# The first q group of the last layer is rounded behind the first splits of the folded projection, and the attention weights lie head by head

## The chip, the cores and the metric

The kernel runs on one core of a Trainium2 chip. The metric is the device time of one execution in microseconds; the time before is the median of three runs.

## What is computed

A two-layer encoder over 272 positions (256 tokens and 16 meta tokens) of width 2048, in float32. Per layer:

```python
h = rmsnorm(x)
q, k, v, f, ga, gf = split(h @ w_in)
q, k = rope_2d(rmsnorm(q)), rope_2d(rmsnorm(k))     # 8 heads of 128, 2 key/value heads
a = attention(q, k, v) @ w_attn_br                  # bidirectional, 4 q heads share one k and v
s = real(fft2(f groups)) @ w_four                   # per group of 128 channels
x = x + (sigmoid(ga) * a + sigmoid(gf) * s) @ w_out
x = x + w_down(silu(dwconv3(rmsnorm(x) @ w_up_gate)) * (rmsnorm(x) @ w_up_val))
```

## The kernel before

**Products in two parts.** A float32 operand is used as a rounded high part and a low part, the difference. A weight chunk of 128 x 1024 (512 KB) is loaded by SyncE into one of four `raw` buffers (L264), ScalarE casts it to the high part `wh` (L306), VectorE subtracts to get the low part `wl` (L308), and TensorE multiplies high by high, high by low and low by high (L377 to L379). `wh` and `wl` have three buffers each. `next_split` and `advance` keep the splits two chunks ahead of the matmuls.

**Work between the matmuls.** Whatever isn't a weight product (norms, rotation, attention) is written as generators that are pushed on a list, `shadow`. After every second product of a group, `step` wakes at most one generator whose count is up; `yield n` sets that count, so a larger n puts the rest of a generator later among the matmuls. A scheduler may then move instructions on an engine; inside `tc.manual_schedule(...)` the engines named keep the written order.

**The last layer's q groups.** `group((l, "q", i), ...)` makes the projection of q group i (two heads). `head_evac` (L927) takes it out of PSUM: the squares on ScalarE (L935, tile `qps`) and the scaled values on VectorE (L936, tile `qp`). `swap` (L946) copies the halves of each head to `qs` by four DMAs. `q_stage` (L1037) takes the sums of squares (the copy L1047 to `sqm` and the transposes L943) and then calls `rope` (L952): two products with sine and cosine (L953, L954), their sum (L955), the rounding to the high part on ScalarE (L956), one `yield`, and the low part on VectorE (L958).

**The folded projection.** Behind q group 1 of the last layer stands `folded_f` (L832), under `manual_schedule` for VectorE and ScalarE. It runs over 16 chunks of a folded weight (`raw<-fw`). For chunk k it first issues the high and low splits of the chunk ahead, then the matmuls of chunk k: for each of four groups g and two halves, high part (L869) and low part (L873), and for the first group two small matmuls besides (L872). The four groups take eight PSUM banks; the third and fourth use the banks of the q groups, the fourth those of q group 1, and its chunk 0 is done within chunk 1 (the list `kg`). Every third chunk up to k = 11 VectorE also makes the folded activations for later chunks (`fold_sum`, `fold_low`). Chunks 0 and 1 are split during the last two chunks of q group 1, chunk 2 at k = 0, chunk 3 at k = 1.

**Attention.** `attention(kv, rq)` handles four heads of one key/value head. Its scores are exponentiated (L1103), normalised (`pn`, L1111 and L1112), transposed on TensorE (L1120) and written, rounded, to `PH` (L1133) and the low part to `PL` (L1134); the third key block holds the meta tokens' remainder, with its low part in rows 32 to 47 (L1136). A head's weights are three key blocks of 272 positions in `PH` and two in `PL`. `values(h)` multiplies them by v: for each of two blocks L1141 (`PH`), L1142 (`PL`) and L1143 (`PH` with the low part of v), and then L1144. In the last layer a head's values are done one round later than the next head's first weights are written. Which earlier write a matmul waits for is found by the framework from the ranges of the tile that the two touch.

## Time and profile before

| | us |
|---|---|
| three runs, median (lowest to highest) | 2510.45 (2509.78 to 2512.84) |
| the profiled execution | 2510.57 |
| its span, first to last instruction | 2508.5 |
| TensorE matmul busy | 2496.9 |
| VectorE busy | 1987.7 |
| ScalarE busy | 1341.0 |
| GpSimd busy | 205.4 |

The span is what the trace covers; the profiled execution's own time is 2.07 us longer. Busy times of different engines overlap. A row of the timeline gives start and duration in microseconds from the start of the span, the engine (PE is TensorE, DVE VectorE, ACT ScalarE, POOL GpSimd, SP SyncE), the source line, the operation, and output and inputs by the program's names; brackets hold the idle time of the engine before it and what ended it. A row of the waits gives the waiting engine and line, what it waited for, and the total, the number of times and the longest. The folded projection runs from 1364.2 to 1399.05 us of the span, and the last layer's attention ends at about 1530.

### The profile page before, as it was taken

What the parts mean: (1) busy time and instruction counts of PE and PEld (TensorE: products, weight loads), DVE (VectorE), ACT (ScalarE), POOL (GpSimd) and SP (SyncE); (2) the same over time, 40 slices, a digit from 0 to 9 for tenths busy, and PEclk for the clock granted to TensorE, in tenths of its full rate; (3) what the DMA queues carried; (4) which work ended last, traced back from release to release, by engine and by line L of the source; (5) the groups of instructions that cost most, each with busy time, mean ns of one, the idle gap of its engine ahead of it and who ended that gap; (6) DMA issues with size and microseconds to landing.
All of it is one profiled execution on the core that took longest, in us unless ns stands there. A gap on an engine that the chain in (4) does not pass through costs nothing.

```text
span 2508.5 us, 47931 instructions
## 1 busy us (share of the span) xinstructions
PE 2496.9 (100%) x18848; PEld 2416.3 (96%) x18848; DVE 1987.7 (79%) x3155; ACT 1341.0 (53%) x1913; POOL 205.4 (8%) x394
## 2 busy tenths in 40 slices
PE   9999999999999999999999999999999999999999
PEld 8999999999999999999999999999988899999887
DVE  7687866778878667888778887666888787898898
ACT  5455434554444334444445555444676665666665
POOL 0000000012212222222200000000000000000000
PEclk9999999999999999999999999999999999999999
DMA  7544557879999999999975647888878887788897
GB/s 249 165 152 164 190 192 245 265 260 377 393 335 383 404 385 377 384 391 389 391 276 197 200 152 236 268 260 273 245 266 294 295 292 237 262 284 291 278 302 272
DMA packets 194803, 706.85 MB, mean 282 GB/s; under 512 B 22145, under 2 KB 27393, under 8 KB 194321
## 3 DMA queue, kind: packets, MB, share of 16 engines
q1 hardware_dynamic: 146768, 517.09, 58.9%
q0 software_dynamic: 46368, 184.57, 21.3%
q8 instruction: 147, 2.41, 0.4%
q10 hardware_dynamic: 1440, 2.13, 0.2%
q14 instruction: 80, 0.65, 0.1%
HBM read 623.32 MB, written 111.15 MB: 293 GB/s over the span
## 4 chain that ended last, share of the span: by engine, by line
PE 98%; DVE 1%; DMA 1%; issue 0%; POOL 0%; ACT 0%; ACTq 0%; DVEq 0%; POOLq 0%
PE ps_p L1455 14%; PE ps_ug L379 7%; PE ps_ug L377 7%; PE ps_ug L378 7%; PE ps_d L379 3%; PE ps_uv L379 3%; PE ps_uv L377 3%; PE ps_uv L378 3%; PE ps_d L377 3%; PE ps_d L378 3%; PE ps_ga L377 2%; PE ps_o L379 2%; PE ps_o L377 2%; PE ps_ga L378 2%; PE ps_ga L379 2%; PE ps_gf L377 2%
## 5 line engine op out<-in xcount | busy, mean ns | idle before, releaser
L306 ACT CAST wh<-raw 128x1024 fp32r<-128x1024 f32 (+1 forms) x961 | 998.3, 1044 | 891.9 <-PE ps_ug L378 194.4
L308 DVE TENSOR_TENSOR wl<-raw,wh 128x1024 fp32r<-128x1024 f32 (+1 forms) x961 | 1158.9, 1217 | 392.3 <-ACT wh L306 382.0
L377 PE MATMUL ps_ug<-xHL,wh 128*128 128x272 f32 (+1 forms) x1408 | 400.4, 285 | 0.0
L379 PE MATMUL ps_ug<-xHL,wl 128*128 128x272 f32 (+1 forms) x1408 | 398.7, 284 | 0.0
L378 PE MATMUL ps_ug<-xHL,wh 128*128 128x272 f32 (+1 forms) x1408 | 398.5, 283 | 0.0
L377 PEld LDWEIGHTS ps_ug<-xHL,wh 128*128 128x128 f32 x1408 | 264.9, 188 | 3.2
L378 PEld LDWEIGHTS ps_ug<-xHL,wh 128*128 128x128 f32 x1408 | 264.5, 188 | 3.2
L379 PEld LDWEIGHTS ps_ug<-xHL,wl 128*128 128x128 f32 x1408 | 264.3, 188 | 1.1 <-DVE wl L308 0.4
L1455 PE MATMUL ps_p<-wh,opnd 128*128 128x512 f32 x816 | 222.1, 392 | 0.0
L379 PE MATMUL ps_uv<-xHL,wl 128*128 128x272 f32 x704 | 201.9, 287 | 0.0
L379 PE MATMUL ps_d<-gHL,wl 128*128 128x272 f32 x704 | 201.7, 287 | 0.0
L377 PE MATMUL ps_uv<-xHL,wh 128*128 128x272 f32 x704 | 201.3, 286 | 0.0
L377 PE MATMUL ps_d<-gHL,wh 128*128 128x272 f32 x704 | 201.1, 286 | 0.0
L378 PE MATMUL ps_uv<-xHL,wh 128*128 128x272 f32 x704 | 200.6, 285 | 0.0
L378 PE MATMUL ps_d<-gHL,wh 128*128 128x272 f32 x704 | 200.6, 285 | 0.0
L1455 PEld LDWEIGHTS ps_p<-wh,opnd 128*128 128x128 f32 x816 | 148.3, 188 | 28.7 <-ACT wh L306 0.2
L377 PE MATMUL ps_ga<-xHL,wh 128*128 128x272 f32 (+1 forms) x512 | 147.8, 289 | 0.0
L540 DVE TENSOR_TENSOR wi<-wi,wi 128x512 f32<-128x512 f32 x224 | 147.0, 685 | 0.0
L377 PE MATMUL ps_gf<-xHL,wh 128*128 128x272 f32 (+1 forms) x512 | 146.7, 287 | 0.0
L379 PE MATMUL ps_o<-mH,wl 128*128 128x272 f32 (+1 forms) x512 | 145.8, 285 | 0.0
L377 PE MATMUL ps_o<-mH,wh 128*128 128x272 f32 (+1 forms) x512 | 145.5, 284 | 0.0
L378 PE MATMUL ps_ga<-xHL,wh 128*128 128x272 f32 (+1 forms) x512 | 145.4, 284 | 0.0
(379 smaller groups left out, 5952.9 us busy)
## 6 DMA issues: line engine op xcount, KB each, us to landing
raw<-in_w_up SPq DMA_DIRECT2D x288, 512.0 KB, 6.5
raw<-in_w_in SPq DMA_DIRECT2D x191, 512.0 KB, 3.8
raw<-in_w_down SPq DMA_DIRECT2D x88, 512.0 KB, 7.0
wi<-in_w_dn POOLq DMA_DIRECT2D x80, 512.0 KB, 9.4
ft<-wi POOLq DMA_DIRECT2D x80, 512.0 KB, 7.7
raw<-ft SPq DMA_DIRECT2D x80, 512.0 KB, 4.7
raw<-in_w_out SPq DMA_DIRECT2D x64, 512.0 KB, 4.3
raw<-fv SPq DMA_DIRECT2D x64, 512.0 KB, 4.8
```

The costliest lines, as they stand in the source:

```text
L306: nc.scalar.copy(h[:, a:b], r[:, a:b])
L308: nc.vector.tensor_tensor(lo[:, a:b], r[:, a:b], h[:, a:b].bitcast(F32), op=ALU.subtract)
L377: nc.tensor.matmul(o, h[:, c, sl], a, start=kt == 0, stop=False)
L378: nc.tensor.matmul(o, h[:, c, sl], b, start=False, stop=False)
L379: nc.tensor.matmul(o, lo[:, c, sl], a, start=False, stop=kt == nk - 1)
L540: tt = lambda *v, **kw: tc.keep_in_program_order(nc.vector.tensor_tensor(*v, **kw))
L1455: nc.tensor.matmul(ps[h], x, w[:, 512 * h:512 * h + 512], start=fresh and (s_, q) in BEGIN and first, stop=(s_, q) in END and end, skip_gr ...
```

## The change

Two edits.

The first concerns q group 0 of the last layer alone. `rope` is cut in two: `turn` is the part up to the sum, and `q_stage` calls only `turn` for that group, after `yield 10` in place of `yield 6`, and leaves the tiles in `hold["q0"]`. The rounding and the low part are issued in `folded_f` at k = 0, behind the splits of the chunk ahead. All other groups call `rope` as before, which now calls `turn`.

The second changes the order of the dimensions of `PH` and `PL` in both layers: (block, head, position) becomes (head, block, position). Shapes, sizes and the instructions are the same.

```diff
                     if k < KT - 1:
                         for j in ahead:
                             split_w(j, 0, CW, "l")
+                    if k == 0:
+                        hp, H, L = hold.pop("q0")
+                        nc.scalar.copy(H, hp)
+                        nc.vector.tensor_tensor(L, hp, H.bitcast(F32), op=ALU.subtract)
                     if k == 13:
                         nc.scalar.activation(warm, mhalf[:, 0:1], AF.Exp)
...
-            def rope(hp, qs, H, L):
+            def turn(hp, qs):
                 tc.keep_in_program_order(nc.vector.tensor_tensor(qs, qs, bc2(sin), op=ALU.mult))
                 tc.keep_in_program_order(nc.vector.tensor_tensor(hp, hp, bc2(cos), op=ALU.mult))
                 nc.vector.tensor_tensor(hp, hp, qs, op=ALU.add)
+
+            def rope(hp, qs, H, L):
+                turn(hp, qs)
                 nc.scalar.copy(H, hp)
                 yield 1
                 nc.vector.tensor_tensor(L, hp, H.bitcast(F32), op=ALU.subtract)
...
-                yield 6 - j
-                yield from rope(qp, qs, qH[kv][:, sl, :], qL[kv][:, sl, :])
+                if last and i == 0:
+                    yield 10
+                    turn(qp, qs)
+                    hold["q0"] = qp, qH[kv][:, sl, :], qL[kv][:, sl, :]
+                else:
+                    yield 6 - j
+                    yield from rope(qp, qs, qH[kv][:, sl, :], qL[kv][:, sl, :])
...
-                PH = PHf.rearrange("p (b h t) -> p b h t", b=3, h=4)
-                PL = PLf[:, :2 * 4 * T].rearrange("p (b h t) -> p b h t", b=2, h=4)
+                PH = PHf.rearrange("p (h b t) -> p b h t", b=3, h=4)
+                PL = PLf[:, :2 * 4 * T].rearrange("p (h b t) -> p b h t", b=2, h=4)
```

How the written order falls out on the engines. The rows give line, operation, output and inputs, and the size of the output; the lines of the changed kernel are its own, up to 13 higher.

VectorE at the seam of q group 1 and the folded projection. `wl_16824` is the low part of chunk 0, `wl_16859` that of chunk 1, `wl_16901` of chunk 2 and `wl_16921` of chunk 3; L953 to L958 rotate and round q group 0 (`q_16735` is its low part), and L936 takes q group 1 out of PSUM. Before:

```order
L308 TENSOR_TENSOR wl_16824<-raw_16651,wh_16823 128x4x256
L953 TENSOR_TENSOR qs<-qs,cst 128x2x272
L954 TENSOR_TENSOR qp<-qp,cst 128x2x272
L955 TENSOR_TENSOR qp<-qp,qs 128x2x272
L958 TENSOR_TENSOR q_16735<-qp,q_16734 128x544
L308 TENSOR_TENSOR wl_16859<-raw_16691,wh_16858 128x4x256
L936 SCALAR_TENSOR_TENSOR qp<-ps_q_0_16743,prm,rstdB 128x258
L936 SCALAR_TENSOR_TENSOR qp<-ps_q_1_16744,prm,rstdB 128x258
L308 TENSOR_TENSOR wl_16901<-raw_16745,wh_16900 128x4x256
L1047 COPY sqm<-qps 128x2x32
L308 TENSOR_TENSOR wl_16921<-raw_16785,wh_16920 128x4x256
```

The same place in the changed kernel, where chunk 1 is `wl_16854` and chunk 2 `wl_16899`:

```order
L308 TENSOR_TENSOR wl_16824<-raw_16651,wh_16823 128x4x256
L308 TENSOR_TENSOR wl_16854<-raw_16691,wh_16853 128x4x256
L957 TENSOR_TENSOR qs<-qs,cst 128x2x272
L958 TENSOR_TENSOR qp<-qp,cst 128x2x272
L1054 COPY sqm<-qps 128x2x32
L959 TENSOR_TENSOR qp<-qp,qs 128x2x272
L940 SCALAR_TENSOR_TENSOR qp<-ps_q_0_16743,prm,rstdB 128x258
L940 SCALAR_TENSOR_TENSOR qp<-ps_q_1_16744,prm,rstdB 128x258
L308 TENSOR_TENSOR wl_16899<-raw_16745,wh_16898 128x4x256
L860 TENSOR_TENSOR q_16735<-qp,q_16734 128x544
L308 TENSOR_TENSOR wl_16921<-raw_16785,wh_16920 128x4x256
```

Chunk 1 has moved ahead of the rotation, the low part of q group 0 behind chunk 2, and the copy of q group 1's squares into the rotation.

ScalarE at the same seam: `wh_16823`, `wh_16858`, `wh_16900` and `wh_16920` are the high parts of chunks 0 to 3, `q_16734` the rounded q group 0, L935 the squares of q group 1. Before:

```order
L306 CAST wh_16823<-raw_16651 128x4x256
L306 CAST wh_16858<-raw_16691 128x4x256
L935 ACTIVATE qps<-ps_q_0_16743 128x258
L956 CAST q_16734<-qp 128x544
L935 ACTIVATE qps<-ps_q_1_16744 128x258
L306 CAST wh_16900<-raw_16745 128x4x256
L306 CAST wh_16920<-raw_16785 128x4x256
```

The same place in the changed kernel:

```order
L306 CAST wh_16823<-raw_16651 128x4x256
L306 CAST wh_16853<-raw_16691 128x4x256
L939 ACTIVATE qps<-ps_q_0_16743 128x258
L939 ACTIVATE qps<-ps_q_1_16744 128x258
L306 CAST wh_16898<-raw_16745 128x4x256
L859 CAST q_16734<-qp 128x544
L306 CAST wh_16920<-raw_16785 128x4x256
```

The rounding has moved from between the two squares to behind chunk 2. The SyncE and GpSimd queues keep their order.

TensorE at the values of the last head but one of the last layer, with the semaphores for which each matmul waits. Before:

```order
L1141 MATMUL ps_pv<-PH,VH 128x258 [waits Activation_49]
L1142 MATMUL ps_pv<-PL,VH 128x258 [waits DVE_49]
L1143 MATMUL ps_pv<-PH,VL 128x258
L1141 MATMUL ps_pv<-PH,VH 128x258
L1142 MATMUL ps_pv<-PL,VH 128x258 [waits DVE_49]
L1143 MATMUL ps_pv<-PH,VL 128x258
L1144 MATMUL ps_pv<-PH,V_83 128x258
```

The same seven in the changed kernel:

```order
L1153 MATMUL ps_pv<-PH,VH 128x258 [waits Activation_49]
L1154 MATMUL ps_pv<-PL,VH 128x258 [waits DVE_49]
L1155 MATMUL ps_pv<-PH,VL 128x258
L1153 MATMUL ps_pv<-PH,VH 128x258
L1154 MATMUL ps_pv<-PL,VH 128x258
L1155 MATMUL ps_pv<-PH,VL 128x258
L1156 MATMUL ps_pv<-PH,V_83 128x258 [waits DVE_49]
```

The second `PL` matmul no longer waits for VectorE; the last of the seven does, for the head's own remainder block.

## The prediction

> **What bounds the kernel now.** I read the page first, then the waits of TensorE alone, then the timeline around each of those waits. Three lines of the page:

> ```profile
> span 2508.5 us, 47931 instructions
> PE 2496.9 (100%) x18848; PEld 2416.3 (96%) x18848; DVE 1987.7 (79%) x3155; ACT 1341.0 (53%) x1913; POOL 205.4 (8%) x394
> ...
> PE 98%; DVE 1%; DMA 1%; issue 0%; POOL 0%; ACT 0%; ACTq 0%; DVEq 0%; POOLq 0%
> ```

> TensorE is busy all the time, and 98% of the chain that ends last is its own work. The change neither adds nor removes a matmul, so the most that it can win is TensorE's idle time, 2508.5 - 2496.9 = 11.6 us less what lies ahead of the first matmul. The waits of TensorE name what is left:

> ```profile
> PE ps_f L444 <- ACT wh L306: 6.0, 2, 4.4
> PE ps_f L873 <- DVE wl L308: 1.1, 1, 1.1
> PE ps_pv L1142 <- DVE PL L1134: 0.6, 1, 0.6
> PE ps_uv L374 <- DVE wl L308: 0.3, 1, 0.3
> ```

> (Columns: total us, times, longest.) The first is the start of the kernel and the last lies in the feed-forward part of the last layer; the change touches neither. The second is the folded projection of the last layer, where the first q group is rounded, and the third the attention of the last layer. So each part of the change has one hole to close.

> **Part one: the rounding moves behind the splits.** TensorE at the start of the folded projection (start, duration, line, operation; in brackets the idle time before):

> ```profile
> 1364.31 0.30 PE L872 MATMUL ps_f<-hA,w64s 128*16 128x138 f32 x2
> 1364.44 0.27 PE L873 MATMUL ps_f<-hA,wl 128*128 128x138 f32 x1
> ...
> 1365.91 0.30 PE L872 MATMUL ps_f<-hA,w64s 128*16 128x138 f32 x2
> 1367.30 0.33 PE L873 MATMUL ps_f<-hA,wl 128*128 128x138 f32 x1 [1.09 <-DVE wl L308]
> ...
> 1368.66 0.33 PE L869 MATMUL ps_f<-hA,wh 128*128 128x276 f32 x1
> ...
> 1368.90 0.34 PE L869 MATMUL ps_f<-hA,wh 128*128 128x276 f32 x1
> ...
> 1369.91 0.28 PE L873 MATMUL ps_f<-hA,wl 128*128 128x138 f32 x1
> ```

> 1364.31 begins chunk 0 and 1365.91 chunk 1. In chunk 0 the low-part matmul L873 starts 0.13 us after L872. In chunk 1 it starts 1.39 us after, because the low part `wl` of chunk 1 isn't there. By starts the hole costs 1.39 - 0.13 = **1.26 us**, more than the 1.09 in brackets, since matmuls overlap and their ends are modelled. [...] By the idle column the two holes of this change would sum to 1.70 us, by starts to 2.04, and the rows here side with starts.

> Why is `wl` late? VectorE in the same microseconds:

> ```profile
> 1360.70 1.22 DVE L308 TENSOR_TENSOR wl<-raw,wh 128x1024 fp32r<-128x1024 f32 x1
> 1362.49 0.73 DVE L953 TENSOR_TENSOR qs<-qs,cst 128x544 f32<-128x544 f32 x1 [0.57 <-DMA qs<-qp]
> 1363.14 0.72 DVE L954 TENSOR_TENSOR qp<-qp,cst 128x544 f32<-128x544 f32 x1
> 1363.89 0.72 DVE L955 TENSOR_TENSOR qp<-qp,qs 128x544 f32<-128x544 f32 x1
> 1365.39 0.73 DVE L958 TENSOR_TENSOR q<-qp,q 128x544 fp32r<-128x544 f32 x1 [0.77 <-ACT q L956]
> 1366.03 1.22 DVE L308 TENSOR_TENSOR wl<-raw,wh 128x1024 fp32r<-128x1024 f32 x1
> 1367.16 0.87 DVE L936 SCALAR_TENSOR_TENSOR qp<-ps_q,prm,rstdB 128x258 f32<-128x258 f32 x2
> 1367.95 1.21 DVE L308 TENSOR_TENSOR wl<-raw,wh 128x1024 fp32r<-128x1024 f32 x1
> 1369.09 0.18 DVE L1047 COPY sqm<-qps 128x64 f32<-128x64 f32 x1
> 1370.39 1.23 DVE L308 TENSOR_TENSOR wl<-raw,wh 128x1024 fp32r<-128x1024 f32 x1 [1.12 <-ACT wh L306]
> ```

> and ScalarE:

> ```profile
> 1361.47 1.05 ACT L306 CAST wh<-raw 128x1024 fp32r<-128x1024 f32 x1 [1.81 <-PE ps_q L378]
> 1362.96 0.39 ACT L935 ACTIVATE qps<-ps_q 128x258 f32<-128x258 f32 x1 [0.44 <-PE ps_q L379]
> 1364.71 0.65 ACT L956 CAST q<-qp 128x544 fp32r<-128x544 f32 x1 [1.36 <-DVE qp L955]
> 1365.26 0.38 ACT L935 ACTIVATE qps<-ps_q 128x258 f32<-128x258 f32 x1
> 1365.54 1.04 ACT L306 CAST wh<-raw 128x1024 fp32r<-128x1024 f32 x1
> 1369.31 2.00 ACT L306 CAST wh<-raw 128x1024 fp32r<-128x1024 f32 x2 [2.74 <-issue]
> ```

> The L308 rows are chunks 0 to 3 in turn. High part and raw data of chunk 1 are there at 1361.47 + 1.05 = 1362.52, but its subtraction stands behind the whole rotation and rounding of q group 0: 0.57 us of waiting for the swapped halves, three products, 0.77 us for ScalarE's rounding, one subtraction. It starts at 1366.03.

> After the change `wl` of chunk 1 follows chunk 0 directly. It waits for its high part and runs from 1362.5 to 1363.7; TensorE needs it at 1364.44 + (1365.91 - 1364.31) = 1366.04. The hole goes: **-1.26 us**. Nothing is added in count: one CAST of 0.65 and one subtraction of 0.73 only change places, and no DMA is moved.

> What is late next? Four things stand behind it, and I date each from the rows, all in the clock of the old trace:
> - The rotation (L953 to L955) starts at 1363.7 instead of 1362.49. The small copy of 0.18 now lies between its second and third product and waits for ScalarE's squares of q group 1. Those no longer stand behind the CAST of q. The last q matmul starts ahead of 1364.31 and takes some 0.28 (the rows of part two), so the second square can run from 1364.6 at the latest to 1365.0, just when VectorE comes to the copy. The rotation ends at 1363.7 + 0.65 + 0.65 + 0.18 + 0.72 = 1365.9.
> - The two evacuations of q group 1 (0.87) end at 1366.8. The fourth folded group takes over their PSUM banks; its first matmul, 1368.66 before, is due at 1368.66 - 1.26 = 1367.40. Margin 0.6.
> - `wl` of chunk 2 ends at 1366.7 + 1.2 = 1367.9 (its high part is cast right behind the squares, by 1366.1). It is due at 1369.91 - 1.26 = 1368.65. Margin 0.75.
> - The CAST of q (0.65, from 1366.1) is over at 1366.8, ahead of the high part of chunk 3, which waits for the matmul of 1368.90 and so starts at 1369.31 - 1.26 = 1368.05 anyway. The late subtraction of q (0.73) fills VectorE from 1367.8 to 1368.6, where it stood waiting before (the 1.12 in front of 1370.39); chunk 3 begins at 1369.1 as it would without it.

> So from chunk 3 on everything stands 1.26 us earlier in the old order, and the cover of the moved pair is VectorE's wait of 1.12. If that cover were gone, the pair would cost up to its 0.73 in front of chunk 3, and 0.5 of the 1.26 would be left.

> **Part two: the weights lie head by head.** TensorE at three of the seven value matmuls of one head, in the order in which they start:

> ```profile
> 1521.15 0.28 PE L1143 MATMUL ps_pv<-PH,VL 128*128 128x258 f32 x1
> 1521.26 0.28 PE L1141 MATMUL ps_pv<-PH,VH 128*128 128x258 f32 x1
> 1522.15 0.39 PE L1142 MATMUL ps_pv<-PL,VH 128*128 128x258 f32 x1 [0.61 <-DVE PL L1134]
> ```

> and VectorE's writes of the weights around it:

> ```profile
> 1517.53 0.42 DVE L1134 TENSOR_TENSOR PL<-ps_pt,PH 128x256 fp32r<-128x256 f32 x1
> 1517.98 0.28 DVE L1136 TENSOR_TENSOR PH<-ps_pt,PH 16x128 fp32r<-16x128 f32 x1
> 1521.52 0.25 DVE L1112 TENSOR_SCALAR pn<-pe,rs 128x48 f32<-128x48 f32 x1
> 1521.69 0.41 DVE L1134 TENSOR_TENSOR PL<-ps_pt,PH 128x256 fp32r<-128x256 f32 x1
> ```

> This L1142, the second `PL` matmul of the head, waits for the write of 1521.69. That is the write of the next head: in the old layout the two key blocks of a head lie 4 x 272 elements apart, and a write to both spans the second block of the head being read. With the blocks of a head side by side this order is gone, and what remains to wait for are the head's own writes, over at 1517.98 + 0.28 = 1518.26. By starts: 1522.15 - 1521.26 = 0.89 against 1521.26 - 1521.15 = 0.11 for its neighbour, so **-0.78 us**. What TensorE needs next from VectorE there, the input `pn` of the next transposes, is written at 1521.52, ahead of the write that it waits for now.

> The writes keep their element counts; only the distance between blocks changes. No row shows such a copy at another distance, so I bound it by the casts of both layers (ns min/median/max):

> ```profile
> L1133 ACT CAST PH<-ps_pt x32: 453/478/483, 141.5 to 1524.8; 128x384 fp32r<-128x384 f32 x32
> L1124 ACT CAST PH<-ps_pt x12: 198/218/230, 137.0 to 1488.6; 128x64 fp32r<-128x64 f32 x12
> ```

> Together 32 x 0.478 + 12 x 0.218 = 18 us. The two forms differ in how their pieces lie and each spreads by 7 to 15% by itself; a tenth more or less would be 1.8 us of ScalarE, which is 53% busy, over two layers and beside matmuls. I take nothing, and half a microsecond either way at TensorE for the range.

> **Sum.** The profiled execution took 2510.57 us, 2.07 outside its span of 2508.5. Span: 2508.5 - 1.26 - 0.78 = 2506.5; time 2508.5. Its 2510.57 lies 0.1 above the median of the three runs (2510.45), so no correction. That is 0.08%; a measurement of this kernel tells about 0.2% (5 us) from no change.

> **Rivals.**
> 1. *VectorE is full there and the hole reopens.* Its breaks between 1360.7 and 1370.4 are few, and the margins above are only 0.6 to 0.75. If the hole comes back at chunk 2 or 3, only part two is won: 2510.57 - 0.78 = 2509.8. Against it: two waits of VectorE (0.57 and 0.77) go at the same time. Chance 0.15.
> 2. *Part two only changes what is waited for*, as ScalarE's `PH` or the next transposes; only 1.26 is won: 2509.3. Chance 0.10.
> 3. *The load is the bound.* The chain of waits puts a load ahead of the late `wl`:

> ```profile
> 1361.95 4.02 DMA raw<-fw
> ```

> If chunk 1 landed at 1365.97 no order would help, and 2509.8 at best, 2510.6 with rival 2. But ScalarE read that chunk at 1361.47. The load begins when `wl` of chunk 0 ends (1360.70 + 1.22 = 1361.92) and frees one of the four buffers, so it is chunk 4's. Chance of no gain from either part, for this or any reason: 0.08.
> 4. *Slower: the small copy in the rotation.* It stands at 1365.0 in VectorE's queue and holds the third product, the evacuations and `wl` of chunk 2 if the squares of q group 1 are late. With a slip S of the rotation TensorE waits S - 0.6 at the banks; at S = 1.9 the first gain is gone, at S = 2.7 both, and 0.2% slower needs about S = 7.7. ScalarE has only one cast of 1.05 that could stand in front, so S over 2.7 would need something no row shows; at S = 4 the time is 2511.9. Chance 0.05.

> The forecast keeps 0.62. Faster by over 0.2% (below 2505.4) would need holes that the waits of TensorE don't have: 0.02, which is drift between runs. Slower by over 0.2% (above 2515.5): 0.04, most of the fourth rival's chance, since what could hold the squares for so long no row bounds. Within: 0.94. The range reaches up to no gain at all with 0.3 of drift, 2510.9, and down by 1.7: 0.7 for drift (the lowest of the three runs lies 0.67 below the median), 0.5 for the copies and 0.5 for small holes that may close by luck (0.3 in L374's wait): 2506.8.

> **What would show it.** TensorE's waits should list L444 and L374 alone. In the timeline L873 of chunk 1 should start 0.13 us after L872, `wl` of chunk 1 should stand in front of the first product of the rotation, and the rounding of q should lie between `wl` of chunks 2 and 3. The second `PL` matmul of every head should follow within 0.13 us of the matmul before it. Wrong would be a new wait of TensorE for `wl` of chunk 2 or 3, or at the first matmul of the fourth folded group, or for a cast of `PH`; and longer `PH` casts, if layout matters.

## The result, and the profile after

| | before, us | after, us |
|---|---|---|
| runs, median (lowest to highest) | 2513.47 (2509.35 to 2516.97), 22 runs | 2508.11 (2506.67 to 2509.43), 22 runs |
| the profiled execution | 2510.57 | 2508.71 |
| its span | 2508.5 | 2506.9 |

The ratio is 0.9981, with a 95% interval of 0.9975 to 0.9987. The time came out as forecast (2508.5), and the span within 0.4 us of the 2506.5 of the sum. But the medians differ by 5.4 us, and the sum has 2.0. The difference lies in the runs of before: nine of the 22 are between 2509.35 and 2511.44, the other thirteen between 2512.84 and 2516.97, and nothing lies between. No run of after is in the upper group. In the experiments below, where the mean granted clock of each run of before is on record, 71 of its 96 runs had a mean clock of 1.000 and 69 of these lay under 2512 (the other two at 2512.15 and 2520.64); the 25 runs with 0.998 or 0.999 lay at 2512.15 and above. So there are two things to explain: the 1.7 us by which after beats the lower group (2509.78, the median of the nine, less 2508.11), and why before has an upper group at all.

Of the page of after, the span and the busy times, which answer to those shown of before:

```profile
span 2506.9 us, 47935 instructions
PE 2497.2 (100%) x18848; PEld 2417.8 (96%) x18848; DVE 1987.6 (79%) x3155; ACT 1340.5 (53%) x1913; POOL 205.5 (8%) x394
```

TensorE is busy as long as before (2497.2 against 2496.9); only its idle time has shrunk. Its waits:

```profile
PE ps_f L444 <- ACT wh L306: 4.5, 1, 4.5
PE ps_uv L379 <- DVE wl L308: 0.7, 1, 0.7
PE ps_kb L997 <- DVE dk L994: 0.5, 1, 0.5
PE ps_uv L374 <- DVE wl L308: 0.3, 1, 0.3
```

Both waits that the change aimed at (L873 before, now L877, and L1142, now L1154) are gone. The 0.7 and the 0.5 stand in code that the change doesn't touch, at 644.89 and 1339.19 us; another execution of the same kernel (in the experiments) has neither. The wait at the kernel's start (L444) differs too, 4.5 here against 6.0, as unrelated to the change.

TensorE at the start of the folded projection and at its last matmul, after:

```profile
1365.00 0.30 PE L876 MATMUL ps_f<-hA,w64s 128*16 128x138 f32 x2
1365.14 0.27 PE L877 MATMUL ps_f<-hA,wl 128*128 128x138 f32 x1
...
1366.60 0.29 PE L876 MATMUL ps_f<-hA,w64s 128*16 128x138 f32 x2
1366.74 0.27 PE L877 MATMUL ps_f<-hA,wl 128*128 128x138 f32 x1
...
1368.04 0.33 PE L873 MATMUL ps_f<-hA,wh 128*128 128x276 f32 x1
...
1369.16 0.29 PE L876 MATMUL ps_f<-hA,w64s 128*16 128x138 f32 x2
1369.29 0.27 PE L877 MATMUL ps_f<-hA,wl 128*128 128x138 f32 x1
...
1398.37 0.23 PE L877 MATMUL ps_f<-hB,wl 128*128 128x138 f32 x1
```

In chunk 1 the low part now follows 1366.74 - 1366.60 = 0.14 behind L876, where it was 1.39. The same last matmul before:

```profile
1398.98 0.23 PE L873 MATMUL ps_f<-hB,wl 128*128 128x138 f32 x1
```

From the first L872/L876 to the last low part the projection took 1398.98 - 1364.31 = 34.67 us before and takes 1398.37 - 1365.00 = **33.37**: 1.30 less, so nothing of the 1.26 is given back later in it.

VectorE at the seam, after:

```profile
1361.82 1.22 DVE L308 TENSOR_TENSOR wl<-raw,wh 128x1024 fp32r<-128x1024 f32 x1
1363.25 1.22 DVE L308 TENSOR_TENSOR wl<-raw,wh 128x1024 fp32r<-128x1024 f32 x1 [0.22 <-ACT wh L306]
1364.91 0.72 DVE L957 TENSOR_TENSOR qs<-qs,cst 128x544 f32<-128x544 f32 x1 [0.43 <-DMA qs<-qp]
1365.55 0.72 DVE L958 TENSOR_TENSOR qp<-qp,cst 128x544 f32<-128x544 f32 x1
1366.19 0.19 DVE L1054 COPY sqm<-qps 128x64 f32<-128x64 f32 x1
1366.30 0.72 DVE L959 TENSOR_TENSOR qp<-qp,qs 128x544 f32<-128x544 f32 x1
1366.94 0.88 DVE L940 SCALAR_TENSOR_TENSOR qp<-ps_q,prm,rstdB 128x258 f32<-128x258 f32 x2
1367.73 1.22 DVE L308 TENSOR_TENSOR wl<-raw,wh 128x1024 fp32r<-128x1024 f32 x1
1368.87 0.72 DVE L860 TENSOR_TENSOR q<-qp,q 128x544 fp32r<-128x544 f32 x1
1369.77 1.23 DVE L308 TENSOR_TENSOR wl<-raw,wh 128x1024 fp32r<-128x1024 f32 x1 [0.18 <-ACT wh L306]
```

Chunk 1 (1363.25) stands ahead of the rotation and waits for its high part alone. The rotation then waits 0.43 for the swapped halves (the four small copies `qs<-qp`): in this execution they landed later than in the one of before, and this order has room for that.

The values of the same head as before, TensorE and then VectorE:

```profile
1520.50 0.28 PE L1153 MATMUL ps_pv<-PH,VH 128*128 128x258 f32 x1
1520.62 0.28 PE L1154 MATMUL ps_pv<-PL,VH 128*128 128x258 f32 x1
```

```profile
1520.91 0.41 DVE L1146 TENSOR_TENSOR PL<-ps_pt,PH 128x256 fp32r<-128x256 f32 x1
```

The second `PL` matmul follows in 0.12 and has begun before the next head's write does. Before, the matmul behind the late one was late as well, 1522.37 - 1522.15 = 0.22 in place of 0.12:

```profile
1522.37 0.29 PE L1143 MATMUL ps_pv<-PH,VL 128*128 128x258 f32 x1
```

In another head of before the second `PL` matmul and the one behind it came 0.22 apart too (1454.69, 1454.91, 1455.13), a wait too short for the list; after has 0.12 there. The casts into the new layout:

```profile
L1145 ACT CAST PH<-ps_pt x32: 457/476/483, 140.5 to 1523.1; 128x384 fp32r<-128x384 f32 x32
L1136 ACT CAST PH<-ps_pt x12: 197/219/231, 136.0 to 1487.8; 128x64 fp32r<-128x64 f32 x12
```

Their medians were 478 and 218 ns. The layout costs nothing.

### The profile page after: what moved, and what is told of

Read it like the earlier page. It is cut to its first block, busy times and chain, and to the rows that moved or that the text cites. A ratio compares the mean times of both kernels' runs of the same rounds, so it can differ in the third digit from the quotient of the medians.

```text
span 2506.9 us, 47935 instructions
## 1 busy us (share of the span) xinstructions
PE 2497.2 (100%) x18848; PEld 2417.8 (96%) x18848; DVE 1987.6 (79%) x3155; ACT 1340.5 (53%) x1913; POOL 205.5 (8%) x394
## 4 chain that ended last, share of the span: by engine, by line
PE 98%; DMA 1%; DVE 1%; issue 0%; ACT 0%; POOL 0%; SPq 0%; DVEq 0%
PE ps_p L1467 14%; PE ps_ug L379 7%; PE ps_ug L377 7%; PE ps_ug L378 7%; PE ps_d L379 3%; PE ps_d L377 3%; PE ps_d L378 3%; PE ps_uv L379 3%; PE ps_uv L377 3%; PE ps_uv L378 3%; PE ps_gf L377 3%; PE ps_ga L377 2%; PE ps_ga L378 2%; PE ps_o L379 2%; PE ps_o L377 2%; PE ps_ga L379 2%
## 5 line engine op out<-in xcount | busy, mean ns | idle before, releaser
L306 ACT CAST wh<-raw 128x1024 fp32r<-128x1024 f32 (+1 forms) x961 | 998.3, 1044 | 885.1 <-PE ps_ug L378 201.7
L308 DVE TENSOR_TENSOR wl<-raw,wh 128x1024 fp32r<-128x1024 f32 (+1 forms) x961 | 1159.0, 1217 | 388.6 <-ACT wh L306 378.4
L379 PE MATMUL ps_ug<-xHL,wl 128*128 128x272 f32 (+1 forms) x1408 | 398.7, 284 | 0.0
L378 PE MATMUL ps_ug<-xHL,wh 128*128 128x272 f32 (+1 forms) x1408 | 398.5, 283 | 0.0
L378 PEld LDWEIGHTS ps_ug<-xHL,wh 128*128 128x128 f32 x1408 | 264.5, 188 | 3.2
L379 PEld LDWEIGHTS ps_ug<-xHL,wl 128*128 128x128 f32 x1408 | 264.3, 188 | 1.1 <-DVE wl L308 0.4
L379 PE MATMUL ps_uv<-xHL,wl 128*128 128x272 f32 x704 | 202.0, 287 | 0.7 <-DVE wl L308 0.7
L379 PE MATMUL ps_d<-gHL,wl 128*128 128x272 f32 x704 | 201.7, 287 | 0.0
L378 PE MATMUL ps_uv<-xHL,wh 128*128 128x272 f32 x704 | 200.6, 285 | 0.0
L378 PE MATMUL ps_d<-gHL,wh 128*128 128x272 f32 x704 | 200.6, 285 | 0.0
L379 PE MATMUL ps_o<-mH,wl 128*128 128x272 f32 (+1 forms) x512 | 145.8, 285 | 0.0
L378 PE MATMUL ps_ga<-xHL,wh 128*128 128x272 f32 (+1 forms) x512 | 145.4, 284 | 0.0
```

The source lines that it names most:

```text
L306: nc.scalar.copy(h[:, a:b], r[:, a:b])
L308: nc.vector.tensor_tensor(lo[:, a:b], r[:, a:b], h[:, a:b].bitcast(F32), op=ALU.subtract)
L378: nc.tensor.matmul(o, h[:, c, sl], b, start=False, stop=False)
L379: nc.tensor.matmul(o, lo[:, c, sl], a, start=False, stop=kt == nk - 1)
```

## The experiments

The first theory is that of the prediction: two holes, one for each part of the change, and nothing else. Its rival is that before loses more at one of the holes than the hole is long. The second and third set test that. Each set was run beside before on the same chip; the last kernel of the third set (the low part made three times) ran later, on another chip, beside before as well.

### Each part alone, and both kernels again

**Only the rounding moved**, the layout as before:

```diff
-                PH = PHf.rearrange("p (h b t) -> p b h t", b=3, h=4)
-                PL = PLf[:, :2 * 4 * T].rearrange("p (h b t) -> p b h t", b=2, h=4)
+                PH = PHf.rearrange("p (b h t) -> p b h t", b=3, h=4)
+                PL = PLf[:, :2 * 4 * T].rearrange("p (b h t) -> p b h t", b=2, h=4)
```

> Only the rounding of q group 0 is moved; the weights lie block by block as before. Theory A (two holes, each worth its time by starts): TensorE's wait at the folded projection is gone, the one at the value matmuls stays at about 0.6; the lowest runs stand 1.26 us below the lowest of the kernel before. Theory B (before has a second level some 4.5 us above its first in about half of its executions, 2509.4 to 2511.4 and 2512.8 to 2517.0 in the 22 runs, and the late split at the folded projection makes it): all runs of this kernel lie within 3 us of each other, the median 3 to 5 us below before. Theory C (the second level comes from the layout): this kernel still shows both levels, and its median is 1.3 us below before at equal mix.

**Only the layout changed**: before with the two lines of the new layout.

> Only the layout of the weights is changed; the rounding stands where it stood. Theory A: the wait at the value matmuls (0.6) is gone, the one at the folded projection (1.1) stays; the lowest runs are 0.78 us below the lowest of before. Theory B: two levels some 4.5 us apart as in before, median about 0.8 below before at equal mix. Theory C: one level only, median 3 to 4 us below before.

**Before and after once more**, unchanged, beside these two:

> The kernel before, unchanged, against itself. All theories: a ratio of 1.000. If two levels exist, the runs of both sides show them, 2509.4 to 2511.4 and 2512.8 to 2517, and a profile of the upper level shows where the 4 to 5 us stand: Theory B says at the folded projection of the last layer (TensorE waits there for 4 us and more instead of 1.1), Theory C at the attention's value matmuls, and a third (drift of the chip or of the loads anywhere) at some other place or spread over many.

> Both parts, unchanged. Theory A: the lowest runs 2.0 us below the lowest of before. Theories B and C: one level only, within 3 us, the median 4 to 5 us below before. If the second level is drift of the chip, this kernel shows it too on a chip where before does.

Runs at a mean clock of 1.000 and below, with medians:

| kernel | runs | ratio to before (95%) | at 1.000 | below 1.000 |
|---|---|---|---|---|
| before (shared by the four) | 35 | | 24, 2509.57 | 11, 2512.94 to 2516.60 |
| before again | 12 | 0.9996 (0.9986 to 1.0005) | 9, 2509.52 | 3, 2513.43 to 2515.52 |
| only the layout | 12 | 0.9995 (0.9986 to 1.0003) | 9, 2508.92 | 3, 2512.62 to 2513.47 |
| only the rounding | 12 | 0.9988 (0.9980 to 0.9996) | 12, 2508.57 | none |
| after again | 12 | 0.9986 (0.9977 to 0.9994) | 12, 2508.05 | none |

TensorE's waits with only the rounding moved:

```profile
PE ps_f L444 <- ACT wh L306: 5.2, 3, 4.4
PE ps_pv L1154 <- DVE PL L1146: 0.6, 1, 0.6
PE ps_uv L374 <- DVE wl L308: 0.3, 1, 0.3
```

and with only the layout changed:

```profile
PE ps_f L444 <- ACT wh L306: 5.0, 2, 4.5
PE ps_f L873 <- DVE wl L308: 1.1, 1, 1.1
PE ps_uv L374 <- DVE wl L308: 0.3, 1, 0.3
PE ps_uv L379 <- DVE wl L308: 0.3, 1, 0.3
```

Each part closes its own hole and leaves the other. Among the runs at 1.000 the rounding brings 2509.57 - 2508.57 = 1.0, the layout 0.65 and both 1.5, beside 1.26, 0.78 and 2.04 of the prediction; single runs scatter by 1 to 2 us, so these don't contradict it. The trace is sharper: the folded projection takes 34.67, 34.81 and 34.72 us in three executions that have the hole (before, before again, only the layout) and 33.37, 33.35 and 33.36 in three that don't (after, only the rounding, after again). From its last low-part matmul to the start of the last value matmul (`ps_pv`) it is 128.9 us in those with the old layout (before, before again, only the rounding) and 127.86 in the three with the new: the layout brings **1.04**, not 0.78.

The table also shows whose the upper group is: the kernels with the hole at the seam have it, those without it don't, whatever the layout. That is theory B of the expectations in kind. Its medians of 3 to 5 us below before did not come (1.6 and 2.1), since only 11 of the 35 runs of before were in the upper group here, against 13 of 22 in the result; how large the group is changes from one set of runs to the next.

### Longer holes

The second theory: behind the hole at the seam TensorE's clock falls in some executions, and that makes the upper group. If so, a longer hole makes the fall more frequent, and a profile shows it. Before, with the low part of q group 0 made twice (and then four times) in front of chunk 1:

```diff
-                nc.vector.tensor_tensor(L, hp, H.bitcast(F32), op=ALU.subtract)
+                for _ in range(times):
+                    nc.vector.tensor_tensor(L, hp, H.bitcast(F32), op=ALU.subtract)
...
-                yield from rope(qp, qs, qH[kv][:, sl, :], qL[kv][:, sl, :])
+                yield from rope(qp, qs, qH[kv][:, sl, :], qL[kv][:, sl, :], 2 if last and i == 0 else 1)
```

> The kernel before, with the low part of q group 0 made twice (the same values again), so that the low part of chunk 1 comes about 0.65 us later and the hole at the seam grows from 1.26 to about 1.9 us by starts. Theory A (holes alone): every run about 0.65 us above before. Theory B, with the mechanism that the first runs suggest (the hole at the seam now and then lets the granted clock drop for some microseconds, mean clock 0.999 instead of 1.000, 4 us): the share of runs at 0.999 rises from about 0.4 to over 0.6, and the level stays 4 to 5 us above the first. If the clock drop has nothing to do with the hole, the share stays at 0.3 to 0.5.

> The kernel before, with the low part of q group 0 made four times, hole about 3.2 us by starts. Theory A: every run 1.95 us above before. Theory B: nearly every run shows the mean clock 0.999 and stands 6 to 7 us above the first level of before; a profile shows where the granted clock drops, at the hole or within a few microseconds behind it, and for how long. If the clock drop is independent of the hole, some runs stay at 1.000.

And the rounding alone, with the hole at the values made longer: the low part of the last head's first block is written three times.

```diff
-                        nc.vector.tensor_tensor(PL[:, :, h, c0:c1], src[:, 0:2], PH[:, 0:2, h, c0:c1].bitcast(F32), op=ALU.subtract)
+                        for _ in range(3 if last and kv == 1 and item == (3, 0) else 1):
+                            nc.vector.tensor_tensor(PL[:, :, h, c0:c1], src[:, 0:2], PH[:, 0:2, h, c0:c1].bitcast(F32), op=ALU.subtract)
```

> The rounding moved as in the change, the old layout of the weights, and the low weights of the last head's first block written three times (the same values again): no hole at the seam, and the hole at the value matmuls grows from 0.77 to about 1.5 to 1.9 us. Theory A: 0.7 to 1.1 us above the kernel with the rounding alone (2508.6 there). Theory B in the form that any hole of this length lets the clock drop: a second level 4 to 5 us up with mean clock 0.999 in some runs. Theory B in the form that it is the seam's own (the hole together with what TensorE does around it): one level only.

| kernel | runs | median (lowest to highest) | ratio to before (95%) | below 1.000 |
|---|---|---|---|---|
| before (shared by the three) | 25 | 2510.06 (2508.65 to 2515.62) | | 4 |
| low part twice | 10 | 2513.66 (2510.85 to 2516.10) | 1.0011 (1.0001 to 1.0020) | 9 |
| low part four times | 10 | 2514.47 (2512.13 to 2519.82) | 1.0017 (1.0007 to 1.0027) | 10 |
| rounding alone, longer hole at the values | 10 | 2509.49 (2508.29 to 2510.95) | 0.9995 (0.9986 to 1.0005) | 1 |

With the low part twice, 0.7 us of work moved the median by 3.6 and all but one run below a mean clock of 1.000. TensorE in its profiled execution:

```profile
1367.06 0.33 PE L873 MATMUL ps_f<-hA,wl 128*128 128x138 f32 x1 [1.78 <-DVE wl L308]
...
1368.66 0.34 PE L869 MATMUL ps_f<-hA,wh 128*128 128x276 f32 x1
...
1368.91 0.53 PE L869 MATMUL ps_f<-hA,wh 128*128 128x276 f32 x1
...
1371.91 0.52 PE L869 MATMUL ps_f<-hA,wh 128*128 128x276 f32 x1
...
1372.33 0.33 PE L869 MATMUL ps_f<-hA,wh 128*128 128x276 f32 x1
```

The same stretch by windows (from and to, length, then the busy time of PE, PEld, DVE, ACT and POOL, the granted clock, the DMA share and GB/s):

```profile
1366.00:1368.00 2.00, 0.94 (x8) 0.94 (x9) 2.00 (x4) 0.00 (x0) 0.00 (x0) 1.00 0.00 0
1368.00:1370.00 2.00, 2.00 (x15) 2.00 (x14) 0.92 (x1) 0.92 (x1) 0.00 (x0) 0.71 0.87 270
1370.00:1372.00 2.00, 2.00 (x12) 1.92 (x11) 1.83 (x2) 1.08 (x2) 0.00 (x0) 0.50 0.75 221
1372.00:1374.00 2.00, 2.00 (x18) 1.97 (x18) 1.97 (x5) 1.25 (x4) 0.00 (x0) 0.93 0.78 227
```

The clock falls to 0.50 at about 1368.9, 1.8 us after TensorE has gone back to work, and is up again by 1372.33, 3.4 us later: the same matmul takes 0.53 instead of 0.34. In this execution the projection takes 1400.10 - 1363.38 = 36.72 us: 2.05 more than before's, 0.69 of them a longer hole (1.78 less 1.09 in the idle column) and 1.36 the fall. So in this execution a hole of 1.78 us was enough for a fall.

With the low part four times the profiled execution (2516.14) has a hole of 5.0, where 1.1 and three times 0.65 make 3.1. TensorE behind the hole and then VectorE:

```profile
1371.42 1.55 PE L873 MATMUL ps_f<-hA,wl 128*128 128x138 f32 x6 [4.95 <-DVE wl L308]
```

```profile
1357.62 0.48 DVE L936 SCALAR_TENSOR_TENSOR qp<-ps_q,prm,rstdB 128x258 f32<-128x258 f32 x1
...
1364.34 0.73 DVE L953 TENSOR_TENSOR qs<-qs,cst 128x544 f32<-128x544 f32 x1 [2.44 <-DMA qs<-qp]
```

The swapped halves came late: 1364.34 - 1358.10 = 6.2 us after the evacuation whose halves they are, while in before it was 4.4 (the evacuation ran from 1357.63 to 1358.11, the product began at 1362.49). In before's order everything behind the rotation waits with it, `wl` of chunk 1 too. (In this kernel five high-part matmuls of chunk 1 also stand ahead of the low part that waits.) The clock is down for twice as long here:

```profile
1370.00:1372.00 2.00, 0.57 (x3) 0.58 (x3) 2.00 (x4) 0.00 (x0) 0.00 (x0) 0.54 0.00 0
1372.00:1374.00 2.00, 2.00 (x11) 2.00 (x11) 1.30 (x2) 0.17 (x1) 0.00 (x0) 0.50 0.73 221
1374.00:1376.00 2.00, 2.00 (x11) 1.92 (x11) 1.09 (x1) 1.82 (x2) 0.00 (x0) 0.50 0.67 205
1376.00:1378.00 2.00, 2.00 (x14) 1.97 (x14) 1.97 (x5) 0.51 (x2) 0.00 (x0) 0.75 0.71 207
```

It falls at about 1370.2, while TensorE still waits, and is up again at about 1377.0. The projection takes 1404.81 - 1363.90 = 40.91: 6.24 more than before's, 3.86 of them the longer hole (4.95 less 1.09) and 2.4 the low clock.

The halves landed late in after's two executions too (1364.91 and, in after again, 1364.12, which is 5.7 and 5.9 us behind their evacuations, with VectorE waiting for them), and TensorE waited for nothing there: `wl` of chunk 1 was done. So in these executions a late landing lengthened the hole in the old order (4.95 where 3.1 was due) and cost nothing in the new one (no wait of TensorE for `wl` of chunk 1 in either). The change isn't needed for it, since the kernel with the low part four times has the old order, and it doesn't always bring it: over the eleven profiles with this swap the slowest of the four copies landed 3.4, 3.7 and 4.0 us after its issue in these three and 2.4 to 2.8 in the other eight, two of which have the new order (the rounding alone, with and without the longer hole at the values).

The longer hole at the values:

```profile
PE ps_pv L1155 <- DVE PL L1147: 1.1, 1, 1.1
```

One of its ten runs lay below 1.000 and none above 2510.95, so a hole of before's length made no upper group at that place. The two kernels with the longer hole at the seam came out as theory B has it in kind, 9 and 10 of 10 runs below 1.000; their medians are 3.9 and 4.7 us above before's runs at 1.000 (2509.75), where 4 to 5 and 6 to 7 were expected.

### The hole without the swap

Is it the short hole or the late swap that sends before to its upper group? Three kernels leave out the swap of q group 0 in the last layer: its tile is filled with a constant, so that no transfer can lengthen the hole.

```diff
-                push(q_stage(i, *qq, swap(qq[0]) if last else None), 1)
+                if last and i == 0:
+                    q0s = rt("qs")
+                    nc.gpsimd.memset(q0s, 0.5)
+                    push(q_stage(i, *qq, q0s), 1)
+                else:
+                    push(q_stage(i, *qq, swap(qq[0]) if last else None), 1)
```

The second and third of these also make the low part twice and three times, as above, which restores a hole of before's length and one of 2 us.

> The kernel before without the four DMAs that swap the halves of q group 0 in the last layer; the swapped tile is filled with a constant instead, so the rotation of that group computes something else. The rotation no longer waits for a DMA and starts about 0.6 us earlier, so the hole at the seam falls to about 0.6 to 0.7 us by starts, and it can't grow where the DMA lands late. Theory D (the upper level is a late swap alone): one level, 0.6 us below before's first. Theory E (the upper level is the clock gate, which a hole of 1.2 us trips in some executions): one level too, since the hole is short. Theory F (drift, neither): a second level as in before in 3 or more of the runs.

> The same without the swap, and the low part of q group 0 made twice: the hole is back at about 1.26 us by starts, as in before, but no DMA can lengthen it. Theory D (late swap alone): one level, at before's first level, mean clock 1.000 throughout. Theory E (clock gate): some runs, a sixth to a half, at mean clock 0.999, and their times in steps of about 1.7 us (one window of half clock, as the 3.4 us at 0.5 in the profile with the hole of 1.9) above the rest. Both together: such runs exist but fewer and lower than in before, at most 3.5 us up.

> Leaves out the swapped halves of q group 0 of the last layer (its tile is filled with a constant) and makes the low part of that group three times. The copy before it, with the low part made twice, had a hole of 1366.85 - 1365.36 - 0.13 = 1.36 us at the seam by starts; one more low part of about 0.65 makes it 2.0, beside the 1.95 of the kernel with the swap and the low part made twice (2510.85 to 2516.10, 9 of 10 runs at a mean clock under 1.000). Theory A, a hole of this length lets the clock fall for one window of 3.4 us, which costs 1.7, and what lies above 2512.6 in the kernels with the swap is the same fall behind a hole that a late swap has made longer still: TensorE's clock is 0.5 for 3.4 us behind the hole, most runs are at a mean clock of 0.999, the times lie at 2510.2 + 0.65 and up to 1.7 more, 2510.9 to 2512.6, and none is at 0.998 or above 2513.2. Theory B, the length of the hole alone decides, and the scatter above 2512.6 is the clock's own: the times scatter as those of the kernel with the swap did, most of them above 2513. Theory C, without the swap a hole of 2.0 does not lower the clock: one level at 2510.9, all at 1.000.

With them before was profiled twice more, for an execution of the upper group:

> The kernel before, one look, in the hope of an execution on its upper level (a third of them). If so: Theory D shows the swap of q group 0 landing over 3 us after its issue and a hole of 2 us and more at the seam with full clock; Theory E a hole of about 1.2 and granted clock 0.5 for 3.4 or 6.8 us behind it; both together a long hole and a clock drop, which add to the 4 us. On the first level: a hole of 1.26 and clock 1.00.

> As the look before it: the kernel before, once more, for an execution on the upper level.

Both fell into the lower group (2510.69 and 2509.47, clock 1.000, `wl` waited for 1.0), so an upper execution of before was never caught in a profile. For the others, TensorE's wait at L873 without the swap:

```profile
PE ps_f L873 <- DVE wl L308: 0.4, 1, 0.4
```

the same wait with the low part made twice:

```profile
PE ps_f L873 <- DVE wl L308: 1.2, 1, 1.2
```

and with the low part made three times:

```profile
PE ps_f L873 <- DVE wl L308: 1.9, 1, 1.9
```

The last of them in the timeline:

```profile
1367.70 0.33 PE L873 MATMUL ps_f<-hA,wl 128*128 128x138 f32 x1 [1.93 <-DVE wl L308]
```

So these holes are 0.4, 1.2 and 1.9 us in the idle column, where before has 1.1 and the kernel with the swap and the low part twice 1.8.

| kernel | wait | runs | median (lowest to highest) | ratio to before (95%) | below 1.000 | above 2513 |
|---|---|---|---|---|---|---|
| no swap | 0.4 | 11 | 2509.61 (2508.78 to 2510.75) | 0.9993 (0.9984 to 1.0002) | 0 | 0 |
| no swap, low part twice | 1.2 | 11 | 2510.21 (2509.33 to 2511.04) | 0.9995 (0.9986 to 1.0003) | 1 (2510.87) | 0 |
| no swap, low part three times | 1.9 | 11 | 2511.50 (2510.29 to 2516.65) | 1.0003 (0.9994 to 1.0012) | 7 | 1 |
| swap, low part twice (above) | 1.8 | 10 | 2513.66 (2510.85 to 2516.10) | 1.0011 (1.0001 to 1.0020) | 9 | 6 |

Without the swap and with the low part once there is one level, which speaks against drift (theory F). Without the swap a hole of before's length leaves no run above 2511.1, while before itself had 11 of 36 runs above 2512.1 beside these three kernels; at that rate eleven runs would all miss it with a chance of (25/36)^11 = 0.02. By the count below 1.000 alone (1 of 11 against 10 of 36) the difference is not clear: one or none of eleven has a chance of 0.15 at that rate. Theory D asked for no run below 1.000 here and theory E for a sixth to a half of them; one of eleven, at 2510.87, is what was put down for both together. With a hole of 1.9 the mean clock was below 1.000 in 7 of 11 runs, but the time then stayed below 2512.3 in all but one: the hole's own 0.65 and one fall of 1.4 on 2510.2 make 2512.2. With the swap six of ten runs of such a hole are above 2513 (on another chip).

So theory A of the last expectation holds but for one run at 2516.65 and 0.998, which it excluded; B (the length alone decides) and C (no fall without the swap) don't. What the runs speak for takes both: a swap that lands late by 1.3 to 1.9 makes before's hole of 1.1 some 2.4 to 3.0 us long, and behind it the clock falls for one or two stretches of 3.4 us. On before's 2509.6 that makes 2509.6 + 1.3 + 1.4 = 2512.3 at least and 2509.6 + 1.9 + 2 x 1.4 = 2514.3 with two; its upper group begins at 2512.15 and ends at 2516.97. That is argued, not caught in a profile, and the run at 2516.65 without a swap and the top of before's group are more than it gives.

In the kernel with the low part three times the profiled execution had the hole of 1.9 and its clock didn't fall: 1.00 in every window of 2 us up to 1376. Holes of about this length went either way here (a fall behind 1.78, none behind 1.93), and the traces show where the two differ. They hold every step of the granted clock. In all fourteen the clock first goes up 8 to 11 us into the span (7.82 in before, 11.19 in after), and its next step down comes a whole number of 3413.3 ns later: 398 and 399 times that in the two with a fall, and 731 to 733 times, when the program ends, in the others (2501.97 us or 733 times in before, 2495.14 us or 731 times in after). The two falls last 3413 and 6827 ns. So in these traces the steps lie on a grid of 3.41 us that does not heed the hole, and it can be laid over each hole (idle column, us):

| kernel (profiled execution) | hole | most of it in one stretch of the grid | clock |
|---|---|---|---|
| low part four times | 4.95 | 3.41, the whole stretch | falls at its end, 1370.17, and stays down in the next, 1.25 of which is idle |
| low part twice | 1.78 | 1.61 | falls at its end, 1368.86 |
| no swap, low part three times | 1.93 | 1.48 | stays |
| no swap, low part twice | 1.19 | 1.19 | stays |
| before, twice more, again, only the layout | 1.02 to 1.24 | 0.69 to 1.02 | stays |

The hole of 1.93 is cut in two by the grid (1.48 and 0.45) and lets the clock stay; the shorter one of 1.78 doesn't. In these executions 1.61 us of idle TensorE within one stretch came with a fall and 1.48 without, one execution each; that the idle time of one stretch decides, with a limit between the two, is inferred from them. From this an estimate, for a limit of 1.55 and a hole anywhere on the grid: a hole of 1.9 reaches it with a chance of (3.41 - 1.9 + 2 x (1.9 - 1.55)) / 3.41 = 0.65 (7 of 11 runs fell), and one of 1.2 not at all (1 of 11). By it before's hole of 1.0 to 1.2 can't reach the limit either, yet 25 of 96 runs fell. Lengthened to 2.4 to 3.0 it does with 0.80 to 0.97, and with late copies in 3 of 11 profiles that gives 0.22 to 0.26, beside 25/96 = 0.26. By this estimate a late swap would account for how often before falls; three profiles are few, and no such execution of before was profiled.

## Why the prediction was right, and what it missed

- **Part one.** The hole went whole, as put: 1.30 by the length of the projection against 1.26. The instructions fell as dated: in the clock of the old trace (0.69 earlier, by the starts of chunk 0) chunk 1's low part began at 1362.56 (said: 1362.5), chunk 3's at 1369.08 (said: 1369.1).
- **The margins.** They were smaller than said, since the swap landed late: the rotation began at 1364.22 in the old clock instead of 1363.7 (with only the rounding moved and no late landing it began at 1363.43, by the starts of chunk 0 1363.69 in the old clock). In after's own clock the evacuations of q group 1 ended at 1367.82, 0.2 ahead of the fourth group's first matmul at 1368.04 (said: 0.6). `wl` of chunk 2 ended at 1368.95, 0.34 ahead of its use at 1369.29 (said: 0.75). The subtraction of q did fill VectorE's wait ahead of chunk 3: 0.18 is left of 1.12. Rival 1 came within 0.2 us, and in none of four profiles of this order (after, after again, the rounding alone, the longer hole at the values) did it happen.
- **Part two.** The wait went and no other took its place, 0.12 between the two matmuls against 0.11 for the neighbour; rival 2 fell. The layout's cost of nothing held. The gain of 0.78 was put too small: 1.04 by the trace. It was taken to the start of the late matmul alone; the 0.1 by which the next one was late besides, and the 0.2 in another head, were left out.
- **The load** (rival 3) is not waited for: chunk 1's low part waits for ScalarE's cast. **The slower rival** had its copy between the second and third product, at 1366.19, and no wait there.
- **The sum** was -2.04 on the span, and the two parts measure 1.30 + 1.04 = 2.3. The two profiled executions differ by 1.6 only: after comes to the projection 0.69 later (four executions of before alone differ by 0.73 there, 1363.58 to 1364.31), is 1.30 faster in it, 1.04 faster from there to the last value matmul, and 0.1 slower behind.
- **The time** of 2508.5 was met partly by luck. The sum stands on one profiled execution, 2510.57, which lay in the lower group, as nine of the 22 runs of before did. What the upper group costs was not in the sum; against the median of before's 22 runs the change is worth 5.4 us.

What was missed is a sentence of the first part: that "the most that it can win is TensorE's idle time". This holds within one execution at full clock. The prediction took one profiled execution for the kernel, and a hole for a loss of its own length, where behind the hole of 1.78 us the fall of the clock cost 1.36 more. Of the three runs shown one (2512.84) already stood apart from the other two by more than 2 us, and the prediction gave it no place. The holes' 2.0 are 0.08%, as said; the ratio of 0.9981 comes from the upper group, which the change removes with the hole at the seam. That the hole is what it hangs on is shown (no run of 46, 34 of after and 12 with only the rounding moved, was below a clock of 1.000). That a late swap lengthens the hole is shown in one profile of a longer hole; that it is the other half of before's upper group the kernels without a swap and the estimate speak for, and for before itself it is only argued. Why some upper runs are as high as 2517 is open: by an estimate from the falls above one stretch of 3.41 us at 0.50 takes 3.41 x 0.50 / 2510 = 0.0007 off the mean clock of a run, so a run at 0.999 had two at most, some 2.8 us, but 2516.60 at 0.999 lies 7 us above the lower group.

## What to carry to other kernels

Here a wait of TensorE could not be priced by its length alone: 0.7 us more of it moved the median by 3.6, with 9 of 10 runs below a mean clock of 1.000, and a late transfer made 4.95 us of a hole where 3.1 was due. Ask of each hole what stands in front of the late instruction: if a transfer does, the hole may differ between executions (the swap here was awaited until 4.3 to 6.2 us behind its evacuation). The order in which that transfer delays only work with room behind it took the scatter away here as well as the mean: the runs of after lie within 2.8 us, those of before within 7.6. When runs of one kernel fall into two groups, put the mean clock of each run beside its time before working with the median.

## What the runs showed of the hardware

The four small copies of 68 KB each between partitions had all landed 4.3 to 4.4 us behind the evacuation that they follow in six executions, and 5.7 to 6.2 us behind it in three others, by the start of the product that waits for them.
